# Gather, prefix sum and matmul on one core: four tiles' indices loaded directly, w loaded and cast in four parts, matmuls on zeros at the start, and the first and last pair of tiles handled singly

## The chip, the core and the metric

The kernel runs on one NeuronCore of a Trainium2 chip. The core has five engines that run their own instruction streams: TensorE (PE), VectorE (DVE), ScalarE (ACT), GpSimd (POOL) and SyncE (SP), and 16 DMA engines that move data between HBM and the on-chip memories. Engines wait for each other through semaphores. The metric is the device time of one execution in microseconds (us), as a median of several runs. A profile is taken of one execution; its "span" is the time from the first to the last instruction of the program, which is a little less than the execution's own time.

## What is computed

```python
B, S, N, D = (16, 4096, 2048, 512)      # x: B,S,D float32; indices: B,N int64, sorted; w: D,D float32
gathered = x[b_idx, indices, :]         # 2048 rows of each of the 16 batches
cs = np.cumsum(gathered, axis=1)        # running sum over the gathered rows, batch by batch
out = np.matmul(cs, w)                  # (16, 2048, 512) float32
```

So 67 MB of rows are read, 67 MB of results are written, and between them stand a running sum down each batch and a product with a 512 x 512 matrix.

## The kernel before, in words

The gathered rows are cut into tiles of 128 rows: 16 tiles to a batch, T = 256 tiles in all. Two neighbouring tiles are a *pair* (R = 2, G = 128 pairs). Each pair goes through these steps, each on its own engine:

- `gather(t)` on POOL: one indirect DMA per tile. 128 row numbers, one to a partition, pick 128 rows of 2 KB, which land in `g32` (eight buffers of a pair). POOL does nothing else after its set-up, so the gathers are issued one behind the other; a gather into a used buffer waits until the pair that was in it has been cast.
- `cast(g)` on ACT: the pair is cast from float32 to float16 (`g16`, four buffers). It waits for both tiles of the pair.
- `sums(t)` on PE: four 128x128 matmuls per tile against `ut`, a matrix of ones and zeros, leave the running sums inside the tile, transposed, in PSUM (`pa`, four buffers).
- `carry(t)` on DVE: adds the last column of the tile before (the total so far) and writes float16 to `cst`; the first tile of a batch is only copied.
- `project(g, j)` on PE: four 128x512 matmuls per tile against `w16` give the output rows in PSUM (`pb`, two buffers of a pair). It waits until both tiles of the pair have been carried and until the buffer has been drained.
- `drain(g)` on ACT: one copy of the pair, 128x1024, from PSUM to `ob` (eight buffers).
- `store(g)` issued by SP: one DMA of 512 KB to the output; each partition writes two neighbouring rows, 4 KB.

The order on each engine is written out by hand. PE runs AH = 2 pairs of sums ahead: it does the sums of pairs 0 and 1, and then `step(g)`: project tile 0 of pair g, sums of tile 0 of pair g+2, project tile 1 of pair g, sums of tile 1 of pair g+2. Most steps run in a loop of four. ACT does cast 0, the cast of w, casts 1 and 2, and then, for every g, cast g+3 and drain g. So the drain of pair g stands behind the cast of pair g+3, which waits for that pair's gathers.

Set-up before that: the row numbers arrive as int64. `idx64` holds the indices of all 256 tiles, one tile to a partition row (two loads of 128 tiles, KI = 2); DVE casts them to float32, PE transposes them, and DVE casts them back to integers in `idxg`, where one tile's indices lie one to a partition. Because this takes a while, the first FIRST = 2 tiles have their indices loaded straight into that form (`idx_first`, 256 separate elements of 8 bytes). w is loaded in one DMA of 1 MB behind the indices on SP's queue, and cast to float16 in one ACT instruction of 128x2048. POOL builds `ident` (for the transposes) and `ut`.

The semaphores that the change touches: `s_first`, `s_w` (landed loads), `s_wc` (w has been cast), `s_prep` (transposed indices ready), `s_c` (pairs cast), `s_b` (tiles projected), `s_d` (tiles carried), `s_e` (pairs drained).

Of the kernel before, what the change touches and what calls it, by code (L numbers as in the profile page):

```python
# [7 lines left out]
P = 128  # L8
FP32 = mybir.dt.float32
FP16 = mybir.dt.float16  # L10
U32 = mybir.dt.uint32
# [16 lines left out]
def kernel(  # L28
# [19 lines left out]
    FIRST = R  # L48
    NG = 16
    NH = 4  # L50
    NA = 4
    NB = 2
    NC = 4
    NO = 8
    LOOP = 4
    AH = 2
# [7 lines left out]
    idx_first = const.tile([P, FIRST, 2], U32)  # L64
# [4 lines left out]
    w16 = const.tile([P, DC, D], FP16)  # L69
    ut = const.tile([P, R, Q], FP16)  # L70
    ident = const.tile([P, P], FP32)
    g32 = [const.tile([P, R, D], FP32, name=f"g32_{i}") for i in range(NG // R)]
    g16 = [const.tile([P, R, D], FP16, name=f"g16_{i}") for i in range(NH)]
    cst = [const.tile([P, DC, R, P], FP16, name=f"cst{i}") for i in range(NC)]
# [6 lines left out]
    def sem(name):  # L81
        return tc.alloc_semaphore(name)

    s_first, s_w, s_ut, s_wc, s_if, s_pt, s_prep = (
        sem(f"s_{n}") for n in ("first", "w", "ut", "wc", "if", "pt", "prep")
    )
    s_idx = [sem(f"s_idx{k}") for k in range(KI)]
    s_g = [sem(f"s_g{i}") for i in range(NG)]
    s_o = [sem(f"s_o{i}") for i in range(NO)]
    s_c = sem("s_c")  # L90
# [8 lines left out]

    def gather(t):  # L100
        g, r = divmod(t, R)
        pool.need(s_c, g + 1 - NG // R)
        if t < FIRST:
            pool.need(s_first, 16)
            ap = idx_first[:, t, 0:1]
        else:
            pool.need(s_prep, t // P + 1)
            ap = idxg[:, t // P, t % P : t % P + 1]
        nc.gpsimd.indirect_dma_start(  # L109
            out=g32[g % (NG // R)][:, r, :],  # L110
            out_offset=None,
            in_=x_flat,
            in_offset=bass.IndirectOffsetOnAxis(ap=ap, axis=0),
            element_offset=(t // NT) * S * D,
        ).then_inc(s_g[t % NG], 16)

    def cast(g):
        for t in range(R * g, R * g + R):
            act.need(s_g[t % NG], 16 * (t // NG + 1))
        act.need(s_a, R * (g - NH + 1))  # L120
        nc.scalar.copy(out=g16[g % NH][:], in_=g32[g % (NG // R)][:]).then_inc(s_c, 1)  # L121

    def sums(t, first=0):
        g, r = divmod(t, R)
        if isinstance(first, int):
            pe.need(s_c, g + 1)
            pe.need(s_ut, 4)
            pe.need(s_d, t - NA + 1)
        elif r == 0:
            nc.tensor.wait_ge(s_c, first + (g + 1))  # L130
# [27 lines left out]

    def project(g, j, first=0):
        if isinstance(first, int):  # L160
            pe.need(s_wc, 1)
            pe.need(s_d, R * (g + 1))
            pe.need(s_e, g - NB + 1)
        elif j == 0:
            nc.tensor.wait_ge(s_d, R * first + R * (g + 1))
            nc.tensor.wait_ge(s_e, first + (g - NB + 1))
        for c in range(DC):
            mm = nc.tensor.matmul(  # L168
                out=pb[g % NB][:, j],
                lhsT=cst[g % NC][:, c, j, :],  # L170
                rhs=w16[:, c, :],
                start=(c == 0),
                stop=(c == DC - 1),
            )
        mm.then_inc(s_b, 1)

    def drain(g):
        act.need(s_o[g % NO], 16 * (g // NO))
        act.need(s_b, R * (g + 1))
        nc.scalar.copy(out=ob[g % NO][:], in_=pb[g % NB][:]).then_inc(s_e, 1)  # L180

    def store(g):
# [2 lines left out]
        sp.need(s_e, g + 1)  # L185
        nc.sync.dma_start(out=dst, in_=ob[g % NO][:]).then_inc(s_o[g % NO], 16)


    with nc.allow_non_contiguous_dma(reason="a few indices, one per partition"):
        nc.sync.dma_start(  # L190
            out=idx_first[:],
            in_=indices[0, 0 : FIRST * P].bitcast(U32).rearrange("(t p w) -> p t w", p=P, w=2),
        ).then_inc(s_first, 16)
    idx_rows = indices.bitcast(U32).rearrange("b (t q) -> (b t) q", q=2 * P)
    for k in range(KI):
        nc.sync.dma_start(
            out=idx64[:, k, :], in_=idx_rows[k * P : (k + 1) * P, :]
        ).then_inc(s_idx[k], 16)
    nc.sync.dma_start(out=w32[:], in_=w.rearrange("(c p) d -> p c d", p=P)).then_inc(s_w, 16)
    for g in range(G):  # L200
        store(g)
    for g in range(G - NO, G):
        sp.need(s_o[g % NO], 16 * (g // NO + 1))


    nc.gpsimd.memset(ident[:], 1.0).then_inc(s_ut, 1)  # L206
# [22 lines left out]
    nc.gpsimd.drain()  # L229


    for k in range(KI):
        dve.need(s_idx[k], 16)
        nc.vector.tensor_copy(out=idxf[:, k, :], in_=idx64[:, k, 0::2]).then_inc(s_if, 1)  # L234
    for k in range(KI):
        pe.need(s_ut, 3)
        pe.need(s_if, k + 1)
        nc.tensor.transpose(  # L238
            out=pb[k % NB][:, 0, :P], in_=idxf[:, k, :], identity=ident[:]
        ).then_inc(s_pt, 1)  # L240
# [24 lines left out]

    cast(0)
    act.need(s_w, 16)
    nc.scalar.copy(out=w16[:], in_=w32[:]).then_inc(s_wc, 1)  # L268
# [36 lines left out]
```

## Time and profile before

| | |
|---|---|
| median of 4 runs | 351.3 us (350.87 to 351.7) |
| the profiled execution, its own time | 350.85 us |
| its span | 349.1 us |
| PE / DVE / ACT / POOL busy | 86% / 51% / 73% / 70% of the span |
| data moved by DMA | 135.66 MB, mean 389 GB/s |
| first gather issued, last gather issued | 3.15 us, 322.13 us |
| first store issued, last store issued | 20.61 us, 344.92 us |

How to read it: a page gives busy times, the DMA rate in 40 equal slices of the span, and the chain of work that ended last. A row of a group reads: line, engine, operation, output <- input, count, then busy time in us and mean ns of one, then idle time in front of the group and what ended it. A row of the timeline reads: start in us, duration in us, engine, line, operation, and in brackets the idle time before it and what ended it; "x4" means that four instructions are merged. "DMA to landing" is the time from the issue of a DMA by its engine to its completion. "issue" is time in which the engine waited for nothing that the profile shows. A stretch row reads: from:to, length, then for each of PE, PE's weight loads, DVE, ACT and POOL the busy us and the number of instructions, then the granted TensorE clock, the mean busy share of the DMA engines, and GB/s. The matmuls' ends are modelled, so a busy PE is not necessarily PE at its peak.

### The profile page before, as it was taken

Reading aid. Unit: us, or ns where it says so; the run is one execution under the profiler, and the core shown is the slowest. Engines: PE = TensorE matmul, PEld = TensorE weight load, DVE = VectorE, ACT = ScalarE, POOL = GpSimd, SP = SyncE. Lnnn points to the kernel's source line nnn. Section 1 sums busy time; section 2 is a strip of 40 time slices with the busy share of each in tenths; the row PEclk is TensorE's granted clock in tenths of the full one; section 3 lists DMA queues with packets and bytes.
Section 4 is the critical chain, followed back from the end, with each engine's and each line's share of the span. In section 5 each row is a group of like instructions: output and inputs, shape, how many; then the busy total and the mean of one; then the engine's idle time right before and its main releaser. Section 6 shows DMA issues by size and latency. Waiting matters only on the chain.

```text
span 349.1 us, 6009 instructions
## 1 busy us (share of the span) xinstructions
PE 299.9 (86%) x2050; PEld 149.8 (43%) x2050; DVE 178.1 (51%) x260; ACT 253.2 (73%) x258; POOL 243.3 (70%) x264
## 2 busy tenths in 40 slices
PE   1398989899989999898898988989889989889883
PEld 0254444445444444444444434445434444445441
DVE  1354555456545555555554545555545555455550
ACT  0765877778778777777777767787778777778763
POOL 6777777777777777777777777777777777777000
PEclk9999999999999999999999999999999999999998
DMA  6789999999999999999999999999999999999945
GB/s 217 231 242 379 408 413 409 413 408 414 416 416 416 416 417 415 416 416 416 417 416 416 416 414 414 407 412 408 413 412 409 417 413 414 413 415 414 390 194 240
DMA packets 40012, 135.66 MB, mean 389 GB/s; under 512 B 6464, under 2 KB 6720, under 8 KB 40000
## 3 DMA queue, kind: packets, MB, share of 16 engines
q0 software_dynamic: 20480, 67.13, 49.3%
q1 hardware_dynamic: 19520, 68.43, 48.6%
q14 instruction: 11, 0.09, 0.1%
q8 instruction: 1, 0.02, 0.0%
HBM read 68.42 MB, written 67.11 MB: 388 GB/s over the span
## 4 chain that ended last, share of the span: by engine, by line
POOL 50%; DMA 23%; issue 19%; PE 3%; ACT 3%; POOLq 0%; SPq 0%; ACTq 0%
POOL g L109 50%; DMA g<-in_x_dram,idxg 22%; ACT g L121 3%; PE pb L168 3%; PE pa L132 1%; DMA idx_first<-in_indices_dram 1%; POOLq L229 0%; ACT ob L180 0%; SPq L300 0%; ACTq L23 0%; SPq L79 0%
## 5 line engine op out<-in xcount | busy, mean ns | idle before, releaser
L109 POOL DMA_INDIRECT g<-in_x_dram,idxg x254 | 240.1, 945 | 77.4 <-issue 72.8
L168 PE MATMUL pb<-w,cst 128*128 128x512 f16 x1024 | 263.4, 380 | 0.0
L152 DVE TENSOR_TENSOR cst<-pa,cst 128x512 f16<-128x512 f32 x240 | 166.0, 692 | 138.9 <-PE pa L132 137.9
L121 ACT CAST g<-g 128x1024 f16<-128x1024 f32 x128 | 133.5, 1045 | 76.3 <-issue 73.7
L132 PE MATMUL pa<-ut,g 128*128 128x128 f16 x1024 | 100.9, 222 | 39.8 <-ACT g L121 38.3
L180 ACT COPY ob<-pb 128x1024 f32<-128x1024 f32 x128 | 128.7, 1005 | 5.2 <-PE pb L168 5.2
L132 PEld LDWEIGHTS pa<-ut,g 128*128 128x128 f16 x1024 | 70.2, 99 | 127.5 <-ACT g L121 94.6
L168 PEld LDWEIGHTS pb<-w,cst 128*128 128x128 f16 x1024 | 89.9, 98 | 61.6 <-issue 0.8
L147 DVE CAST cst<-pa 128x512 f16<-128x512 f32 x16 | 11.1, 692 | 19.7 <-PE pa L132 19.7
L121 ACT ACT_TABLE_LOAD x1 | 1.3, 1283 | 10.2 <-DMA g<-in_x_dram,idx_first 10.2
L238 PE MATMUL pb<-ident,idxf 128*128 128x128 f32 x2 | 0.9, 462 | 4.1 <-DVE idxf L234 4.0
L109 POOL DMA_INDIRECT g<-in_x_dram,idx_first x2 | 2.1, 1042 | 1.5 <-DMA idx_first<-in_indices_dram 1.2
L234 DVE CAST idxf<-idx 128x128 f32<-128x128 uint32 x2 | 0.5, 226 | 4.1 <-DMA idx<-in_indices_dram 4.1
L238 PEld LDWEIGHTS pb<-ident,idxf 128*128 128x128 f32 x2 | 0.4, 182 | 4.4 <-issue 4.0
L268 ACT CAST w<-w 128x2048 f16<-128x2048 f32 x1 | 1.9, 1893 | 0.0
L243 DVE CAST idxg<-pb 128x128 uint32<-128x128 f32 x2 | 0.6, 291 | 0.3 <-PE pb L238 0.3
L206 POOL MEMSET ident<- 128x128 f32 x1 | 0.2, 204 | 0.5 <-SPq L79 0.5
L209 POOL TENSOR_SCALAR_AFFINE_SELECT ident<-ident 128x128 f32<-128x128 f32 x1 | 0.3, 286 | 0.1
L289 POOL MEMSET const-float32-0.0<- 128x1 f32 x1 | 0.1, 98 | 0.3 <-issue 0.3
L218 POOL TENSOR_SCALAR_AFFINE_SELECT ut<-ut 128x128 f16<-128x128 f16 x1 | 0.3, 289 | 0.0
L207 POOL MEMSET ut<- 128x128 f16 x1 | 0.2, 205 | 0.0
L289 POOL MEMSET const-uint8-127<- 128x1 uint8 x1 | 0.1, 115 | 0.0
(2 smaller groups left out, 0.2 us busy)
## 6 DMA issues: line engine op xcount, KB each, us to landing
out_dram<-ob SPq DMA_DIRECT2D x128, 512.0 KB, 7.1
g<-in_x_dram,idxg POOLq DMA_INDIRECT x254, 10.1
w<-in_w_dram SPq DMA_DIRECT2D x1, 1024.0 KB, 6.3
idx<-in_indices_dram SPq DMA_DIRECT2D x2, 128.0 KB, 2.2
g<-in_x_dram,idx_first POOLq DMA_INDIRECT x2, 5.5
idx_first<-in_indices_dram SPq DMA_DIRECT2D x1, 2.0 KB, 1.9
```

Of the source, the lines that this page charges most:

```text
L109: nc.gpsimd.indirect_dma_start(out=g32[g % (NG // R)][:, r, :], out_offset=None, in_=x_flat, in_offset=bass.IndirectOffsetOnAxis(ap=ap, ax ...
L121: nc.scalar.copy(out=g16[g % NH][:], in_=g32[g % (NG // R)][:]).then_inc(s_c, 1)
L132: mm = nc.tensor.matmul(out=pa[t % NA][:, c], lhsT=g16[g % NH][:, r, c * P : (c + 1) * P], rhs=ut[:], start=(c == 0), stop=(c == DC - 1),)
L147: nc.vector.tensor_copy(out=dst, in_=pa[t % NA][:]).then_inc(s_d, 1)
L152: nc.vector.tensor_tensor(out=dst, in0=pa[t % NA][:], in1=last.unsqueeze(2).broadcast_to([P, DC, R, Q]), op=mybir.AluOpType.add,).then_inc ...
L168: mm = nc.tensor.matmul(out=pb[g % NB][:, j], lhsT=cst[g % NC][:, c, j, :], rhs=w16[:, c, :], start=(c == 0), stop=(c == DC - 1),)
L180: nc.scalar.copy(out=ob[g % NO][:], in_=pb[g % NB][:]).then_inc(s_e, 1)
L209: nc.gpsimd.affine_select(out=ident[:], in_=ident[:], compare_op=mybir.AluOpType.is_equal, fill=0.0, base=0, pattern=[[-1, P]], channel_mu ...
L234: nc.vector.tensor_copy(out=idxf[:, k, :], in_=idx64[:, k, 0::2]).then_inc(s_if, 1)
L238: nc.tensor.transpose(out=pb[k % NB][:, 0, :P], in_=idxf[:, k, :], identity=ident[:]).then_inc(s_pt, 1)
L243: nc.vector.tensor_copy(out=idxg[:, k, :], in_=pb[k % NB][:, 0, :P]).then_inc(s_prep, 1)
L268: nc.scalar.copy(out=w16[:], in_=w32[:]).then_inc(s_wc, 1)
```

## The change

At the start:
- FIRST becomes 4: the indices of tiles 0 to 3 are loaded straight, in two loads, tiles 0 and 1 by SP's queue and tiles 2 and 3 by ACT's, each with its own semaphore.
- w is loaded in four DMAs of 256 KB, each with its own semaphore. ACT casts the first two parts and DVE the last two, each 128x512; a projection waits for all four.
- DVE first clears a small tile `zeros`; PE multiplies it with itself nine times ahead of the transposes and ten times behind them, into a PSUM buffer that nobody reads. ACT copies one column of `zeros` to `spare` before anything else.
- Pair 0 is cast as two single tiles, each with its own step of the new semaphore `s_c0`; the sums of tile 0 wait only for tile 0.
- The cast of w stands ahead of the first gathered tile on ACT, no longer behind it. PE does the sums of pair 0, then the projections of pair 0 alternating with the sums of pair 1, then the sums of pair 2, then the steps from pair 1 on.

At the end:
- The last pair is cast as two single tiles (`s_c1`).
- PE does both projections of pair 125 ahead of the sums of tile 254, and one projection of pair 126 between the sums of tiles 254 and 255.
- The last pair is drained in halves, 128x512 each, tile 254 by DVE and tile 255 by ACT, and stored in two DMAs of 256 KB with rows of 2 KB.

Between start and end the loop is as before; only the counts of `s_c` are shifted by one.

```diff
-    FIRST = R
+    FIRST = 2 * R
...
+    zeros = const.tile([P, D], FP16)
+    spare = const.tile([P, 1], FP16)
...
     def gather(t):
         g, r = divmod(t, R)
-        pool.need(s_c, g + 1 - NG // R)
+        if g >= NG // R:
+            pool.need(s_c0, R)
+            pool.need(s_c, g - NG // R)
         if t < FIRST:
-            pool.need(s_first, 16)
+            pool.need(s_first[g], 16)
...
+    def cast_tile(t, done):
+        g, r = divmod(t, R)
+        act.need(s_g[t % NG], 16 * (t // NG + 1))
+        act.need(s_a, R * (g - NH + 1))
+        nc.scalar.copy(out=g16[g % NH][:, r], in_=g32[g % (NG // R)][:, r]).then_inc(done, 1)
...
-            pe.need(s_c, g + 1)
+            if g in (0, G - 1):
+                pe.need(s_c1 if g else s_c0, r + 1)
+            else:
+                pe.need(s_c, g)
...
-            pe.need(s_wc, 1)
+            pe.need(s_wc, DC)
...
+    def drain_last(j, lane, copy):
+        g = G - 1
+        lane.need(s_o[g % NO], 16 * (g // NO))
+        lane.need(s_b, R * g + j + 1)
+        copy(out=ob[g % NO][:, j], in_=pb[g % NB][:, j]).then_inc(s_el[j], 1)
+
+    def store_last():
+        b, h = divmod(G - 1, GB)
+        dst = out[b, h * R * P : (h + 1) * R * P, :].rearrange("(p j) d -> p j d", j=R)
+        for j in range(R):
+            sp.need(s_el[j], 1)
+            nc.sync.dma_start(out=dst[:, j], in_=ob[(G - 1) % NO][:, j]).then_inc(s_ol[j], 16)
...
-        nc.sync.dma_start(
-            out=idx_first[:],
-            in_=indices[0, 0 : FIRST * P].bitcast(U32).rearrange("(t p w) -> p t w", p=P, w=2),
-        ).then_inc(s_first, 16)
+        for k, eng in enumerate((nc.sync, nc.scalar)):
+            t = k * R
+            eng.dma_start(
+                out=idx_first[:, t : t + R, :],
+                in_=indices[0, t * P : (t + R) * P]
+                .bitcast(U32)
+                .rearrange("(t p w) -> p t w", p=P, w=2),
+            ).then_inc(s_first[k], 16)
...
-    nc.sync.dma_start(out=w32[:], in_=w.rearrange("(c p) d -> p c d", p=P)).then_inc(s_w, 16)
-    for g in range(G):
+    for c in range(DC):
+        nc.sync.dma_start(out=w32[:, c, :], in_=w[c * P : (c + 1) * P, :]).then_inc(s_w[c], 16)
+    for g in range(G - 1):
         store(g)
+    store_last()
...
+    def busy(n):
+        pe.need(s_z, 1)
+        for _ in range(n):
+            nc.tensor.matmul(
+                out=pb[NB - 1][:, R - 1], lhsT=zeros[:, :P], rhs=zeros[:], start=True, stop=True
+            )
+
+    nc.vector.memset(zeros[:], 0.0).then_inc(s_z, 1)
...
+    busy(9)
     for k in range(KI):
         pe.need(s_ut, 3)
...
+    busy(10)
...
+    for c in range(DC // 2, DC):
+        dve.need(s_w[c], 16)
+        nc.vector.tensor_copy(out=w16[:, c, :], in_=w32[:, c, :]).then_inc(s_wc, 1)
     for t in range(T):
         carry(t)
+    drain_last(0, dve, nc.vector.tensor_copy)
...
-    for t in range(R * AH):
+    for t in range(R):
         sums(t)
     pe.need(s_prep, KI)
-    for g in range(LOOP):
+    for j in range(R):
+        project(0, j)
+        sums(R + j)
+    for t in range(2 * R, R * (AH + 1)):
+        sums(t)
+    for g in range(1, LOOP):
         step(g)
...
-    for g in range(G - LOOP, G):
+    for g in range(G - LOOP, G - AH - 1):
         step(g)
-
-
-    cast(0)
-    act.need(s_w, 16)
-    nc.scalar.copy(out=w16[:], in_=w32[:]).then_inc(s_wc, 1)
+    project(G - 3, 0)
+    project(G - 3, 1)
+    sums(T - 2)
+    project(G - 2, 0)
+    sums(T - 1)
+    project(G - 2, 1)
+    project(G - 1, 0)
+    project(G - 1, 1)
+
+
+    act.need(s_z, 1)
+    nc.scalar.copy(out=spare[:], in_=zeros[:, :1])
+    for c in range(DC // 2):
+        act.need(s_w[c], 16)
+        nc.scalar.copy(out=w16[:, c, :], in_=w32[:, c, :]).then_inc(s_wc, 1)
+    for t in range(R):
+        cast_tile(t, s_c0)
     for g in range(1, AH + 1):
         cast(g)
-    for g in range(G):
-        if g + AH + 1 < G:
+    for g in range(G - 1):
+        if g + AH + 1 < G - 1:
             cast(g + AH + 1)
+        elif g + AH + 1 == G - 1:
+            for t in range(T - R, T):
+                cast_tile(t, s_c1)
         drain(g)
+    drain_last(1, act, nc.scalar.copy)
```

More of the change, by code (lines that the diff above doesn't have):

```diff
@@ L82, in sem @@
         return tc.alloc_semaphore(name)
-    s_first, s_w, s_ut, s_wc, s_if, s_pt, s_prep = (
-        sem(f"s_{n}") for n in ("first", "w", "ut", "wc", "if", "pt", "prep")
-    )
+    s_z, s_ut, s_wc, s_if, s_pt, s_prep, s_c0, s_c1 = (
+        sem(f"s_{n}") for n in ("z", "ut", "wc", "if", "pt", "prep", "c0", "c1")
+    )
+    s_first = [sem(f"s_first{k}") for k in range(2)]
+    s_w = [sem(f"s_w{c}") for c in range(DC)]
     s_idx = [sem(f"s_idx{k}") for k in range(KI)]
+    s_el = [sem(f"s_el{j}") for j in range(R)]
+    s_ol = [sem(f"s_ol{j}") for j in range(R)]
     s_g = [sem(f"s_g{i}") for i in range(NG)]
@@ L129, in sums @@
         elif r == 0:
-            nc.tensor.wait_ge(s_c, first + (g + 1))
+            nc.tensor.wait_ge(s_c, first + g)
         for c in range(DC):
@@ L198 @@
         ).then_inc(s_idx[k], 16)
-    nc.sync.dma_start(out=w32[:], in_=w.rearrange("(c p) d -> p c d", p=P)).then_inc(s_w, 16)
-    for g in range(G):
+    for c in range(DC):
+        nc.sync.dma_start(out=w32[:, c, :], in_=w[c * P : (c + 1) * P, :]).then_inc(s_w[c], 16)
+    for g in range(G - 1):
         store(g)
-    for g in range(G - NO, G):
+    store_last()
+    for g in range(G - NO, G - 1):
         sp.need(s_o[g % NO], 16 * (g // NO + 1))
+    for j in range(R):
+        sp.need(s_ol[j], 16)
     nc.gpsimd.memset(ident[:], 1.0).then_inc(s_ut, 1)
@@ L252, in step @@
                 sums(R * (g + AH) + j, first)
-    for t in range(R * AH):
+    for t in range(R):
         sums(t)
     pe.need(s_prep, KI)
-    for g in range(LOOP):
+    for j in range(R):
+        project(0, j)
[3 more added lines that the diff above has]
+    for g in range(1, LOOP):
         step(g)
```

## The prediction

> **What bounds the kernel now.** I read the page's slices and the chain first, then the landing times of the gathers at four places, then both ends in order of time.
>
> ```profile
> GB/s 217 231 242 379 408 413 409 413 408 414 416 416 416 416 417 415 416 416 416 417 416 416 416 414 414 407 412 408 413 412 409 417 413 414 413 415 414 390 194 240
> POOL 50%; DMA 23%; issue 19%; PE 3%; ACT 3%; POOLq 0%; SPq 0%; ACTq 0%
> L109 POOL DMA_INDIRECT g<-in_x_dram,idxg x254 | 240.1, 945 | 77.4 <-issue 72.8
> ```
>
> The chain says POOL: 256 gathers, one every 1.25 us (0.95 busy, 0.30 issue), the first at 3.15 us, the last at 322.13. But the rate row says more. A pair of tiles is read (524,288 B) and written (524,288 B); at one pair per 2.5 us that asks for 419 GB/s, and the DMA moves 407 to 417. So it serves slightly less than POOL orders, and a queue must grow. It does: these are the landing times of gathers issued in 8 to 20, 24 to 50, 100 to 120 and 300 to 349 us.
>
> ```profile
> DMA to landing us min/median/max: 3.5/3.7/4.7
> DMA to landing us min/median/max: 6.5/7.7/8.0
> DMA to landing us min/median/max: 8.0/8.5/8.8
> DMA to landing us min/median/max: 14.4/14.8/15.6
> ```
>
> From 3.7 us with an empty queue to 15.6 at the end. The trace also records the sixteen partial completions of each gather: fifteen parts of the last one are in by 329.1 us and the sixteenth at 337.7. One of the 16 DMA engines is the last, and nothing in steady state waits for anything else.
>
> So the end is: the moment the DMA becomes fully loaded, plus the work in front of the last read, plus a tail. Before stores exist, the DMA is half idle (last column GB/s, the one before it the DMA's share):
>
> ```profile
> 12.00:16.00 4.00, 1.70 (x15) 1.44 (x16) 1.41 (x3) 4.00 (x4) 2.99 (x4) 1.00 0.70 216
> 16.00:20.00 4.00, 4.00 (x22) 2.06 (x20) 2.25 (x4) 1.59 (x3) 3.09 (x4) 1.00 0.71 210
> 20.00:24.00 4.00, 4.00 (x32) 2.32 (x31) 2.56 (x4) 3.57 (x5) 3.09 (x4) 1.00 0.89 261
> ```
>
> The first store is late because of this stretch: table load, cast 0, the whole of w on ACT, three casts, a slow first projection, the first drain.
>
> ```profile
> 10.19 1.28 ACT L121 ACT_TABLE_LOAD   x1 [10.19 <-DMA g<-in_x_dram,idx_first]
> 11.48 1.04 ACT L121 CAST g<-g 128x1024 f16<-128x1024 f32 x1
> 12.44 1.89 ACT L268 CAST w<-w 128x2048 f16<-128x2048 f32 x1
> 14.23 2.93 ACT L121 CAST g<-g 128x1024 f16<-128x1024 f32 x3
> 16.16 1.91 PE L168 MATMUL pb<-w,cst 128*128 128x512 f16 x4
> 19.58 1.01 ACT L180 COPY ob<-pb 128x1024 f32<-128x1024 f32 x1 [2.41 <-PE pb L168]
> 20.61 13.91 SPq L186 DMA_DIRECT2D out_dram<-ob  x6
> ```
>
> Check of the reading: store data flows from about 22.5 us (first store issued at 20.6, data 1.9 later). From there to the last landing at 337.7 are 315.2 us. In them lie 243 reads of 262,144 B and 123 stores of 524,288 B; at 414 GB/s these take 243 x 0.633 + 123 x 1.266 = 309.6 us, 98% of it. That stretch has almost no slack to lose or gain; only where it begins, and the tail, can move.
>
> **The change part by part.**
>
> *Four tiles' indices straight.* POOL's third gather already starts at 5.85 us with no wait beyond its 0.30, so this removes nothing; it moves the first use of the transposed indices from tile 2 (5.85) to tile 4 (8.35). The second load goes by ACT's queue beside SP's first. The first load's 8-byte packets ran from 2.09 to 2.54 us, so sharing can cost the first gather between 0 and 0.45; each packet took 9 ns, 16 to an engine, which leaves room, so I take 0.1.
>
> *Nineteen matmuls on zeros, transposes behind nine of them.* The DVE memset that they wait for lies between 0.20 us (POOL's memset of 128x128) and 0.69 (a DVE cast of 128x512): 0.4, ending at 1.4. Nine at the cold 0.43 to 0.48 us (1.91 for four at 16.16) end at 5.4 to 5.8. Two transposes (0.46 each) and one index cast (0.29) put the first indices at 6.2 to 6.6 against 8.35: 1.7 us of cover, cost nothing; were it gone, POOL's chain would slip one for one. Ten more end between 8.8 and 11; the first prefix sums can start at 10.1. What PE could lose there is below 1 us and is covered by 2 us (below).
>
> *w in four loads, casts on ACT and DVE.* SP issues three DMAs more, 0.43 to 0.47 us each, all before its first store. w was complete at 8.8 us and is the same bytes. ACT's two casts (a 1024-wide one takes 1.05, a 2048-wide one 1.89, so 0.62 each for 512) and DVE's two end near 9.5, when the first gather has just landed whole (9.46); the table load goes to the idle front. DVE's two casts run while POOL writes gathers. In the trace the one gather with such a DVE cast inside it (3.64) took 1.14 us, its neighbours 0.95: 0.19 for a cast of 0.23. Bounds: 0, and both casts in full, 2 x 0.69 = 1.4. I take the row, 0.2 in all, since it isn't certain that both fall inside a gather. The Trainium skill's "SBUF — State Buffer" (section "SBUF: two separate sides") warns that such a DVE copy locks GpSimd out, so that gathers cannot be written for its whole length; by that rule alone the term would be up to its upper end, 1.4, and the forecast 350.0.
>
> *First pair by single tiles, and the start.* Casts 0, 1, pair 1 and pair 2 now follow the landings (9.46, 10.12, 11.5, 13.7 us), and projection 0 ends near 14.2. On ACT the cast of pair 3 stands ahead of drain 0, so drain 0 waits for tile 7, which is issued at 12.10 and lands at 15.71 whatever the others do: 15.75 + 1.05 + 1.0 = 17.8, against 20.6. That is the 2 us of cover. From there store g follows the landing of pair g+3 by 2.05 us, as it does before from store 4 on (29.64, 31.66).
> Stores begin 2.8 us earlier, but reads are paced by POOL: 2.8/1.25 = 2.2 reads are still to come, 1.4 us of DMA work. The last landing moves by 2.8 - 1.4 = 1.4 us. Bounds: 0 (the DMA finds other holes, as in 24 to 28 us at 314 GB/s) and 2.8 (the whole shift). Less the two delays (0.1 + 0.2): 1.1.
>
> *Last pair by single tiles.* Times after the last landing L, before: cast 0.07 to 1.12, last sums to 2.65, two projections of pairs 126 and 127 to 6.12, drain to 7.2, store issued 7.23, its last packet 9.5, end of the span 11.4. After: tile 254 lands 1.2 us ahead and is cast before L; tile 255 is cast at 0.07 to 0.69; drain 124 then ends at 1.6 and frees the buffer for projection 126, whose first half runs 1.75 to 2.6; sums 255 to 2.85, second half to 3.7, projection 127 to 5.45. The halves are drained by DVE (4.65 to 5.35) and ACT (5.5 to 6.1), where before it was one copy of 1.01. The last store is issued at 6.15, 1.1 us sooner. It is half the size, but store 126 and the first half are still ahead of it: data ends near 8.1 instead of 9.5. Gain 1.4 (bounds 1.1, the issue alone, and 1.7, no queue).
>
> Between the ends the loop is the same, instruction for instruction, with counts shifted by one. **Sum:** 1.1 + 1.4 = 2.5 us. The profiled execution took 350.85 (span 349.1); the median of the four, 351.3, is 0.45 more, and the same 2.5 comes off it: **348.8 us**.
>
> **The rivals.**
>
> *Only the tail gains (349.9).* If the DMA isn't as continuously loaded as I say, earlier stores only fill holes that would have been filled later, and L stays: 351.3 - 1.4. For it: 24 to 28 us moved 314 GB/s with gathers already waiting 7.5 us. Against: the 98%.
>
> *The queue never builds (346.8).* Before, four drains came every 2.17 us (19.58, 21.75, 23.92, 26.10) and the landing time jumped from 3.7 to 7.5. After, they come at the reads' own 2.5 us. If that spares the jump, L moves by the whole 2.8, and with 1.7 in the tail: 351.3 - 4.5.
>
> *Slower: the transposes come late.* They stand behind nine matmuls in PE's queue, and gather 4 at 8.35 us and all later ones stand behind them. Cover is 1.7 us, and each us beyond it delays every gather. Against a gain of 2.5, it ends over 0.2% slower once the first indices are 1.7 + 2.5 + 0.7 = 4.9 us late, that is if nine matmuls take 8.9 us, 1.0 each. At 1.0 each: 352.0. The rows show 0.43 to 0.48, so this needs a price twice theirs.
>
> *No change:* the idle before the first store turns out to be hidden and the tail's gain is lost in stores queued in front of it: 351.0.
>
> **How the numbers follow.** 0.2% is 0.7 us, about what a measurement of this kernel can tell from none. My case 0.55; tail alone 0.19; no queue 0.12; no change 0.06; slower 0.08. Faster: 0.55 + 0.12 + 0.17 of the tail case (349.9 is near the border) = 0.84; same 0.08; slower 0.08. The range takes in the tail case with its smaller end (351.3 - 1.1 = 350.2, and 0.2 for the median's own scatter) and the no-queue case: 346.6 to 350.4.
>
> **What would show it.** Right: gathers start at 3.1 to 3.3 us and keep 1.25; the first store is issued near 17.8; gathers issued from 24 to 50 us land in 5.5 to 6.5 us instead of 7.7, those from 300 us in 13 to 14.5; from the last cast's end to the last store's issue 5.5 us instead of 6.1. Wrong: the first store after 19.5, a wait of POOL at tile 4, landings unchanged at 24 to 50 us (then only the tail can gain), or another engine that lags by more than 8.6 us.

## The result: no change that can be measured

The kernel after takes 351.4 us (median of 34 runs, 350.15 to 352.99), the kernel before 351.17 (55 runs, 350.31 to 352.65). The ratio is 1.0007, 95% interval 0.9999 to 1.0016. The forecast was 348.8 us, with a range that ended at 350.4. The profiled execution of after took 351.93 us (span 350.1), 0.5 over its own median; that of before took 350.85, 0.3 under its own. Where two single profiles are compared below, these differences have to be kept in mind.

The page of after, in the lines that answer to those shown of before: the DMA rate in 40 slices, the chain, the gathers.

```profile
GB/s 229 207 295 357 386 392 397 411 411 416 418 415 416 416 415 414 413 416 414 416 415 416 412 410 411 411 414 413 412 414 416 411 415 412 409 411 415 389 202 241
POOL 51%; DMA 25%; issue 18%; ACT 2%; PE 2%; POOLq 0%; SPq 0%; ACTq 0%
L117 POOL DMA_INDIRECT g<-in_x_dram,idxg x252 | 238.3, 946 | 76.8 <-issue 71.6
```

The third slice is faster (295 GB/s against 242), as the earlier stores should make it. But slices four to seven read 357, 386, 392, 397, where before had 379, 408, 413, 409. What was won in one slice was given back in four.

The time from issue to landing of the gathers issued in 8 to 20, 24 to 50, 100 to 120 and 300 to 349 us, kernel after:

```profile
DMA to landing us min/median/max: 3.5/3.7/6.5
DMA to landing us min/median/max: 5.6/8.2/9.2
DMA to landing us min/median/max: 9.4/9.8/10.1
DMA to landing us min/median/max: 15.2/16.2/16.7
```

The forecast asked for 5.5 to 6.5 us in the second line and 13 to 14.5 in the last. Both medians went up instead: from 7.7 to 8.2, and from 14.8 to 16.2.

The start itself went as planned. First the beginning of after in order of time, then what ACT does around the first stores:

```profile
1.47 4.02 PE L273 MATMUL pb<-zeros 128*128 128x512 f16 x9 [1.47 <-DVE zeros L277]
1.47 1.28 ACT L332 ACT_TABLE_LOAD   x1 [1.47 <-SPq L81]
3.36 1.14 POOL L117 DMA_INDIRECT g<-in_x_dram,idx_first  x1 [1.39 <-DMA idx_first<-in_indices_dram]
...
5.74 0.50 DVE L291 CAST idxg<-pb 128x128 uint32<-128x128 f32 x2 [1.08 <-PE pb L285]
...
7.13 0.43 DVE L294 CAST w<-w 128x512 f16<-128x512 f32 x1 [0.89 <-DMA w<-in_w_dram]
7.31 1.06 POOL L117 DMA_INDIRECT g<-in_x_dram,idx_first  x1 [0.30 <-issue]
...
8.66 0.48 DVE L294 CAST w<-w 128x512 f16<-128x512 f32 x1 [1.10 <-DMA w<-in_w_dram]
8.68 0.95 POOL L117 DMA_INDIRECT g<-in_x_dram,idxg  x1 [0.30 <-issue]
```

The table load lies in idle time, the transposed indices come in time, and the gather at 8.68, the first that needs them, has no wait beyond its usual 0.30. The first store is issued at 17.97 us instead of 20.61:

```profile
15.98 1.04 ACT L129 CAST g<-g 128x1024 f16<-128x1024 f32 x1 [1.22 <-DMA g<-in_x_dram,idxg]
16.94 1.00 ACT L197 COPY ob<-pb 128x1024 f32<-128x1024 f32 x1
18.64 1.04 ACT L129 CAST g<-g 128x1024 f16<-128x1024 f32 x1 [0.70 <-issue]
19.59 1.00 ACT L197 COPY ob<-pb 128x1024 f32<-128x1024 f32 x1
22.02 1.04 ACT L129 CAST g<-g 128x1024 f16<-128x1024 f32 x1 [1.42 <-issue]
22.97 1.00 ACT L197 COPY ob<-pb 128x1024 f32<-128x1024 f32 x1
26.62 1.04 ACT L129 CAST g<-g 128x1024 f16<-128x1024 f32 x1 [2.64 <-issue]
27.57 1.00 ACT L197 COPY ob<-pb 128x1024 f32<-128x1024 f32 x1
```

This view shows where the lead is lost. Each drain (COPY) follows a cast, and before each cast ACT is idle: 1.22, 0.70, 1.42 and 2.64 us. The cast at 26.62 is that of pair 6, tiles 12 and 13. The bracket says "issue", a wait that the profile can't name; the completions in the trace can: the last part of tile 13 lands at 26.55. In before it landed at 24.31, with its gather issued 0.33 us earlier, and the gather of tile 12 took 3.5 us there and 6.5 here, where two stores had been issued by then. So the stores, in us of issue, go:

| store | 1st | 2nd | 3rd | 4th | 5th | 6th | 7th | 8th | 9th | 10th |
|---|---|---|---|---|---|---|---|---|---|---|
| before | 20.61 | 22.79 | 24.96 | 27.14 | 31.69 | 34.19 | 36.86 | 38.73 | 41.42 | 44.04 |
| after | 17.97 | 20.62 | 24.0 | 28.6 | 30.54 | 33.18 | 35.04 | 38.52 | 43.6 | 46.22 |

The lead of 2.64 us has become a lag of 1.5 at the fourth store, comes back, and is a lag of 2.2 at the ninth and tenth. Before, pair 6 had landed (24.31) well ahead of the fourth store, so the first four stores follow each other every 2.17 us without waiting for a gather; the first such gap there is behind the fourth.

Stretches of 8 us (after 8 to 20), first after, then before; the last two columns are the mean busy share of the DMA engines and GB/s:

```profile
8.00:20.00 12.00, 7.60 (x59) 3.78 (x58) 6.01 (x9) 6.64 (x8) 8.95 (x11) 1.00 0.78 227
20.00:28.00 8.00, 4.72 (x36) 2.32 (x34) 2.77 (x4) 3.94 (x5) 6.17 (x7) 1.00 0.98 335
28.00:36.00 8.00, 7.94 (x60) 4.26 (x57) 4.85 (x8) 6.33 (x7) 6.05 (x7) 1.00 1.00 346
36.00:44.00 8.00, 4.45 (x30) 2.15 (x29) 2.76 (x4) 3.91 (x4) 5.99 (x7) 0.99 1.00 395
44.00:52.00 8.00, 8.00 (x49) 4.24 (x47) 4.05 (x6) 6.87 (x7) 6.17 (x7) 0.80 1.02 386
```

```profile
8.00:20.00 12.00, 5.70 (x34) 3.51 (x35) 3.66 (x6) 7.39 (x7) 8.95 (x11) 1.00 0.76 238
20.00:28.00 8.00, 8.00 (x59) 4.50 (x58) 5.18 (x8) 6.46 (x7) 6.17 (x7) 1.00 0.92 288
28.00:36.00 8.00, 6.04 (x43) 2.84 (x41) 3.62 (x6) 5.04 (x6) 5.87 (x8) 1.00 0.99 380
36.00:44.00 8.00, 7.68 (x55) 4.03 (x56) 4.50 (x7) 6.60 (x7) 6.17 (x7) 1.00 1.03 409
44.00:52.00 8.00, 7.10 (x50) 3.46 (x49) 4.21 (x7) 5.88 (x7) 5.97 (x7) 1.00 1.02 411
```

A DMA share of 1.00 is not full speed: at 28 to 36 us after shows 1.00 at 346 GB/s. The packets take longer. From 32 to 36 us a 4 KB packet of a gather took 233 ns on average in after and 184 in before, and from 100 us on, in before, it takes about 160. At 159 ns, the median there, 16 engines move 412 GB/s. So I count for each stretch the *hole*, its length times (1 - rate/412), and add the stretches from 8 to 80 us. Before has 8.27 us (5.07 of it up to 20 us, 3.20 behind), after 9.32 (5.39 and 3.93). The kernel with the earlier first store has the larger hole.

The rows of after hold a second difference: the granted TensorE clock is 0.80 from 44 to 52 us and 1.00 in before. A slower clock could delay stores too. But the fourth and the ninth store of after, at 28.60 and 43.6 us, are late ahead of that stretch. (In only the start, one of the kernels below, the clock is 0.57 from 28 to 36 us, but its late fourth store, at 30.45, waits for tile 13, which lands at 28.40.) And of the 36 executions of after on record, the seven with a mean clock of 0.997 or more, which leaves hardly any room for a dip, have a median of 351.4 us, as all have. (The twelve at 0.989 or less have 351.95, so part of the scatter may come from the clock.)

### The profile page after: what moved, and what is told of

Same layout as the page of the kernel before. It is cut to its first block, busy times and chain, and to the rows that moved or that the text cites. A ratio compares the mean times of both kernels' runs of the same rounds, so it can differ in the third digit from the quotient of the medians.

```text
span 350.1 us, 6060 instructions
## 1 busy us (share of the span) xinstructions
PE 304.9 (87%) x2069; PEld 152.0 (43%) x2069; DVE 180.1 (51%) x264; ACT 253.0 (72%) x262; POOL 243.5 (70%) x264
## 4 chain that ended last, share of the span: by engine, by line
POOL 51%; DMA 25%; issue 18%; ACT 2%; PE 2%; POOLq 0%; SPq 0%; ACTq 0%
POOL g L117 51%; DMA g<-in_x_dram,idxg 24%; ACT g L129 2%; PE pb L185 2%; DMA idx_first<-in_indices_dram 1%; PE pa L149 0%; ACT ob L209 0%; POOLq L267 0%; SPq L373 0%; ACTq L23 0%; SPq L81 0%
## 5 line engine op out<-in xcount | busy, mean ns | idle before, releaser
L129 ACT CAST g<-g 128x1024 f16<-128x1024 f32 x126 | 131.7, 1045 | 83.4 <-issue 78.0
L273 PE MATMUL pb<-zeros 128*128 128x512 f16 x19 | 6.6, 516 | 1.5 <-DVE zeros L277 1.5
L117 POOL DMA_INDIRECT g<-in_x_dram,idx_first x4 | 4.1, 1023 | 2.3 <-DMA idx_first<-in_indices_dram 1.4
L273 PEld LDWEIGHTS pb<-zeros 128*128 128x128 f16 x19 | 2.3, 127 | 4.6 <-issue 2.2
L135 ACT CAST g<-g 128x512 f16<-128x512 f32 x4 | 2.5, 619 | 1.8 <-DMA g<-in_x_dram,idx_first 1.5
L335 ACT CAST w<-w 128x512 f16<-128x512 f32 x2 | 1.2, 617 | 2.9 <-DMA w<-in_w_dram 2.9
L294 DVE CAST w<-w 128x512 f16<-128x512 f32 x2 | 0.9, 452 | 2.0 <-DMA w<-in_w_dram 2.0
```

What stands on the lines that cost most here:

```text
L117: nc.gpsimd.indirect_dma_start(out=g32[g % (NG // R)][:, r, :], out_offset=None, in_=x_flat, in_offset=bass.IndirectOffsetOnAxis(ap=ap, ax ...
L135: nc.scalar.copy(out=g16[g % NH][:, r], in_=g32[g % (NG // R)][:, r]).then_inc(done, 1)
L273: nc.tensor.matmul(out=pb[NB - 1][:, R - 1], lhsT=zeros[:, :P], rhs=zeros[:], start=True, stop=True)
L335: nc.scalar.copy(out=w16[:, c, :], in_=w32[:, c, :]).then_inc(s_wc, 1)
```

## The experiments

The question was whether the earlier first store brought nothing at all, or brought its gain and something else took it back. Two kernels take the halves of the change apart; two move the first store by holding PE back. They ran on one chip, with 29 runs of the kernel before (351.3 us) beside them.

**Only the end (e1_tail_only).** The kernel before with the single-tile casts and half drains of the last pair, and PE's order at the end; the start is before's.

```diff
+    project(G - 3, 1)
+    sums(T - 2)
+    project(G - 2, 0)
+    sums(T - 1)
...
+    drain_last(1, act, nc.scalar.copy)
```

> The kernel before with only the end of the change. Theory A (the head start of the stores is given back before 60 us, and only the tail gains): 0.5 to 0.9 us faster than before, since after the last landing the changed kernel needed 10.7 us where before needed 11.4. Theory B (the last landing follows from when the DMA gets its full load, as I predicted): the same here, 0.5 to 1.4 us faster, with the last landing unchanged at 336.5 to 338.5 us. If it isn't faster at all, the tail's gain is no gain.

Measured: 350.69 us (12 runs, 350.14 to 351.24), ratio 0.9983 (0.9971 to 0.9994). The end alone gains 0.6 us (0.2 to 1.0 by the interval), and no other version here has a lower median. Both theories asked for such a time, so this run does not part them; the last landing, 338.76 us, lies just above the range of theory B.

**Only the start (e2_start_only).** The kernel after with before's end.

```diff
-    for g in range(G - 1):
-        if g + AH + 1 < G - 1:
+    for g in range(G):
+        if g + AH + 1 < G:
...
-    drain_last(1, act, nc.scalar.copy)
```

> The changed kernel with the end of before. Theory A: no gain, 0 to 1.2 us slower than before (the whole change measured +0.2 with the tail's gain of some 0.7 in it); the store lead of 2.6 us at the first store is gone by the eighth. Theory B: 1.1 us faster than before.

Measured: 352.27 us (12 runs), ratio 1.0027 (1.001 to 1.0043). The start alone loses 1.0 us (0.4 to 1.5 by the interval), as theory A had it; theory B, a gain of 1.1, is out. With the 0.6 of the end that makes +0.4, and the whole change measured +0.2: the halves add up, and nothing takes the start's gain back later. It has none.

**The first store put back by PE alone (e3_late45).** More matmuls on zeros stand ahead of the first sums; all else of the start stays.

```diff
-    busy(10)
+    busy(45)
```

> The changed kernel with 45 in place of 10 matmuls on zeros behind the transposes, so that the first projections and with them the first store come some 3 us later, near 21 us, about where they were before. Theory A: within 0.5 us of the changed kernel, slower or faster. Theory B: 1.4 us slower than the changed kernel (3 us less store time, half of it DMA work).

Measured: 351.82 us (12 runs), ratio 1.0009 (0.9993 to 1.0026). That is 0.4 us over after's 351.4, within theory A's 0.5 and not theory B's 1.4. The first store is issued at 20.70 us, where before has it. Its stretches are before's again as well:

```profile
20.00:28.00 8.00, 7.66 (x58) 4.21 (x56) 6.05 (x9) 6.39 (x7) 6.17 (x7) 1.00 0.93 293
28.00:36.00 8.00, 7.86 (x57) 4.14 (x56) 4.82 (x8) 6.03 (x7) 5.87 (x8) 1.00 1.00 390
36.00:44.00 8.00, 6.93 (x49) 3.44 (x48) 4.05 (x7) 5.87 (x6) 6.17 (x7) 1.00 1.02 398
```

and the last gather lands at 337.81 us, as before's does (337.69). By that the kernel should have been about as quick as the one with the end alone, yet it took 1.1 us more. In its profile the loss is behind the last landing. The DMA from 340.5 to 349 us:

```profile
q1 hardware_dynamic: 692, 1.98, 59.5%
q8 instruction: 1, 0.02, 0.7%
issues: line engine op xcount, KB each, median us to landing
out_dram<-ob SPq DMA_DIRECT2D x2, 512.0 KB, 4.6
out_dram<-ob SPq DMA_DIRECT2D x2, 256.0 KB, 4.0
```

One packet of 16 KB of instructions is fetched at 341.5 us and takes 0.96 us on one DMA engine. The sixteenth part of each of the last four stores then comes 1.4 to 2.5 us behind the fifteenth, where the other five profiles show at most 0.04; the two half stores land in 4.0 us, not 2.6. The next two store packets that take longer than 200 ns, at 342.41 and 342.83 us, take 441 and 249 ns instead of about 160. With the fetch that is 1.3 us lost, and the very last part is 1.36 us late. The other kernels of this section fetch only once, at 22 to 30 us, with the one of the next test as the exception (23.8 and 41.5). The Trainium skill's "Runtime: NRT & Kernel Launch" (section "Terms") says that an engine's instruction memory is refilled in 16 KiB blocks; the packet has that size. That one engine did all three, and that the fetch delayed the stores, is read from these times; that the 35 more matmuls caused the fetch is not shown. No kernel was run that moves the fetch alone.

**The first store put back further (e4_late70).** As above with `busy(70)`.

> The same with 70 matmuls on zeros: first store near 26 us, 8 us later than in the changed kernel. Theory A: at most 1.5 us slower than the changed kernel, because PE and ACT then work off the pairs in a burst that fills the DMA. Theory B: 4 us slower.

Measured: 353.73 us (6 runs), ratio 1.0073 (1.0051 to 1.0095), +2.4 us over before and +2.3 over after. The first store is issued at 25.37 us. Its stretches from 20 to 36 us:

```profile
20.00:28.00 8.00, 6.21 (x53) 3.65 (x52) 5.11 (x8) 2.50 (x3) 6.17 (x7) 1.00 0.75 217
28.00:36.00 8.00, 8.00 (x60) 4.45 (x59) 5.23 (x8) 7.28 (x8) 5.87 (x8) 1.00 1.00 346
```

The measured +2.3 lies between the figures that the expectation gives for the two theories, and fits neither. So a late first store does cost time; an early one does not give it back. Now the profiles side by side, in us. "Last landing" is the last part of the last gather; "at the median" adds to it by how much the kernel's median differs from its profiled execution's time, which assumes that this difference arises before the landing. "Tile 12" is the time from issue to landing of its gather.

| kernel | first store | tile 12 | hole | last landing | at the median |
|---|---|---|---|---|---|
| before | 20.61 | 3.5 | 8.27 | 337.69 | 338.0 |
| only the end | 21.85 | 3.7 | 8.52 | 338.76 | 338.2 |
| after | 17.97 | 6.5 | 9.32 | 339.39 | 338.9 |
| only the start | 18.11 | 8.5 | 9.38 | 339.37 | 338.8 |
| e3_late45 | 20.70 | 4.5 | 8.24 | 337.81 | 338.0 |
| e4_late70 | 25.37 | 3.6 | 10.27 | 340.40 | 341.3 |

The last landing follows the hole: their difference is 329.4 to 330.2 in all six. (The hole was defined after the fact and is bookkeeping: it says how much time the DMA lost, not why.) Against the first store it has a lowest point, near 20.7 us, with a loss on both sides. Single landings scatter, as the second row shows, whose start is before's and whose landing is 1.1 us later; put to the median the three with a first store at 20.6 to 21.9 agree within 0.2 us, and the two at 18 within 0.1. POOL's later beginning (3.36 us instead of 3.15 in after) isn't the cause: only the start has 3.18 and the same last landing, and e3_late45 has 3.27 and before's.

The sixteen partial completions of a gather show which part of the DMA this is. Microseconds from the issue of a gather to its fifteenth and to its last part:

```
tile      24         64         96         128        192        255
before    5.9  7.4   7.4  8.0   8.5  8.7   8.6 10.1   7.2 13.3   7.0 15.6
after     7.4  9.1   8.0  8.6   7.5 10.1   7.6 11.1   6.9 14.3   6.9 16.9
```

Fifteen parts come within 6 to 9 us at tile 24 and still at tile 255; in these two kernels no queue grows on them. Only one falls behind, all the way. I read a part as the work of one of the 16 engines: after 329 us in before, the gathers' last 24 packets of 4 KB run one behind the other, never two at once. After's extra lag on this part (10.1 against 8.7) is there by tile 96 and is then kept to the end (1.0 to 1.4 us). On this reading the fifteen make up what they lose early, and the one never does. But the lag alone does not tell the kernels apart. Only the end, which starts as before does, shows 9.7 us at tile 96 and 16.4 at tile 255. At tile 255 the last part is behind the fifteenth by 8.6 us in before, 9.8 in only the end, 9.9 in after, 9.8 in only the start, 9.2 in e3_late45 and 8.1 in e4_late70, where the fifteenth itself takes 10.1. Nothing in the trace tells which engine moved a packet, so the hole above is that of all sixteen, a stand-in for that of the one.

**What stayed open.** Four more edits were to show directly whether the DMA's work sets the landing (half of every store left out), whether the order of ACT makes the hole (for the first eight pairs the drain ahead of the next cast), whether the second load queue and DVE's casts matter (both index loads on SP, all casts of w on ACT), and whether a burst of stores with the first ones held back does better (`hold`).

```diff
-        nc.sync.dma_start(out=dst, in_=ob[g % NO][:]).then_inc(s_o[g % NO], 16)
+        nc.sync.dma_start(out=dst[:, 0], in_=ob[g % NO][:, 0]).then_inc(s_o[g % NO], 16)
...
-        sp.need(s_e, g + 1)
+        sp.need(s_e, max(g + 1, 2))
```

The first pair of lines is the half store, the second the hold of two; the hold of three has a 3. The other two edits are told in words above.

Half the store, four times:

> The changed kernel, but of every pair but the last only the first of each partition's two rows is stored (half of the output stays unwritten). If the load of the DMA sets the last landing, then with three quarters of the bytes the gathers land 3.5 to 5 us after their issue to the end, the last one at 326 to 328 us, and the span is 337 to 340 us. If POOL or the processing chain set it, the span stays within 3 us of 350.

> The changed kernel, but of every pair but the last only the first of each partition's two rows is stored (half of the output stays unwritten). If the load of the DMA sets the last landing, then with three quarters of the bytes the gathers land 3.5 to 5 us after their issue to the end, the last one at 326 to 328 us, and the span is 337 to 340 us. If POOL or the processing chain set it, the span stays within 3 us of 350.

> The changed kernel, but of every pair but the last only the first of each partition's two rows is stored (half of the output stays unwritten). If the load of the DMA sets the last landing, then with three quarters of the bytes the gathers land 3.5 to 5 us after their issue to the end, the last one at 326 to 328 us, and the span is 337 to 340 us. If POOL or the processing chain set it, the span stays within 3 us of 350.

> The changed kernel, but of every pair but the last only the first of each partition's two rows is stored (half of the output stays unwritten). If the load of the DMA sets the last landing, then with three quarters of the bytes the gathers land 3.5 to 5 us after their issue to the end, the last one at 326 to 328 us, and the span is 337 to 340 us. If POOL or the processing chain set it, the span stays within 3 us of 350.

The drain ahead of the cast, twice:

> The changed kernel, but for the first eight pairs ACT drains pair g ahead of casting pair g+3, so that a finished pair's store does not wait for later gathers to land: first store near 15.8 us, 2 us earlier still. Theory A1 (the lead is lost because stores then wait for gathers, stop and go): fewer holes in the DMA between 28 and 60 us, and 0.5 to 1.5 us faster than the changed kernel. Theory A2 (a lead makes the load so even that the queue of gathers runs short, whatever the order on ACT): no faster than the changed kernel, within 0.5 us, or slower.

> The changed kernel, but for the first eight pairs ACT drains pair g ahead of casting pair g+3, so that a finished pair's store does not wait for later gathers to land: first store near 15.8 us, 2 us earlier still. Theory A1 (the lead is lost because stores then wait for gathers, stop and go): fewer holes in the DMA between 28 and 60 us, and 0.5 to 1.5 us faster than the changed kernel. Theory A2 (a lead makes the load so even that the queue of gathers runs short, whatever the order on ACT): no faster than the changed kernel, within 0.5 us, or slower.

One queue for the index loads and all casts of w on ACT, four times:

> The changed kernel without the two things that held POOL up by 0.2 to 0.35 us: the second index load goes by SP's queue behind the other index loads, and ACT casts all four parts of w. First gather back at 3.15 us, the fifth at 8.35. If those delays explain the start's loss of 1 us, it is 0.8 to 1.1 us faster than the changed kernel; if they only shift the gathers, 0.2 to 0.35 us faster; by theory A the rest of the loss stays.

> The changed kernel without the two things that held POOL up by 0.2 to 0.35 us: the second index load goes by SP's queue behind the other index loads, and ACT casts all four parts of w. First gather back at 3.15 us, the fifth at 8.35. If those delays explain the start's loss of 1 us, it is 0.8 to 1.1 us faster than the changed kernel; if they only shift the gathers, 0.2 to 0.35 us faster; by theory A the rest of the loss stays.

> The changed kernel without the two things that held POOL up by 0.2 to 0.35 us: the second index load goes by SP's queue behind the other index loads, and ACT casts all four parts of w. First gather back at 3.15 us, the fifth at 8.35. If those delays explain the start's loss of 1 us, it is 0.8 to 1.1 us faster than the changed kernel; if they only shift the gathers, 0.2 to 0.35 us faster; by theory A the rest of the loss stays.

> The changed kernel without the two things that held POOL up by 0.2 to 0.35 us: the second index load goes by SP's queue behind the other index loads, and ACT casts all four parts of w. First gather back at 3.15 us, the fifth at 8.35. If those delays explain the start's loss of 1 us, it is 0.8 to 1.1 us faster than the changed kernel; if they only shift the gathers, 0.2 to 0.35 us faster; by theory A the rest of the loss stays.

The kernel after once more beside them, twice:

> The changed kernel once more, for a second profile: how far the last landing and the holes in the DMA's work before 80 us scatter from one execution to the next. If the last landing follows the holes, it is 329.8 us plus the time that the DMA lost between 8 and 80 us, to within 0.5 us.

> The changed kernel once more, timed beside the others and for a second profile: how far the last landing and the holes in the DMA's work before 80 us scatter from one execution to the next. If the last landing follows the holes, it is 329.8 us plus the time that the DMA lost between 8 and 80 us, to within 0.5 us.

The first stores held back:

> The changed kernel, but SP sends the first store only when two pairs are drained, so stores 0 and 1 go together near 20.6 us instead of 17.97 and 20.62. Theory A: although one store is 2.6 us later, the holes before 80 us shrink from 9.3 to 8.3 to 9 us, and it is 0 to 1 us faster than the changed kernel. Theory B (every store earlier is a gain): 1.3 us slower than the changed kernel.

> The same with three pairs: stores 0, 1 and 2 go together near 23 us. Theory A: within 1 us of the changed kernel on either side. Theory B: 2.5 us or more slower than the changed kernel (5 and 2.5 us of delay for the first two stores, half of it DMA work).

These runs fell on chips where the kernel before itself took 440 to 465 us instead of 351, and so they say nothing on the question. There the granted clock was 0.87 to 0.90 in the profiled executions, against 0.98 to 1.00 above, and the last gather landed 4.5 to 6.7 us after its issue, not 16. In us, medians (each half store is one execution):

| edit | this | before beside it |
|---|---|---|
| half store (e5, e9, e13, e16) | 454.9, 457.6, 449.1, 462.6 | 455.9, 457.3, 451.1, 456.6 |
| drain first (e6, e10) | 456.3, 454.1 | 455.9, 457.3 |
| quiet (e7, e11, e14, e15) | 461.2, 460.8, 456.2, 454.9 | 455.9, 457.3, 457.3, 456.6 |
| after again (e8, e12) | 460.9, 457.4 | 455.9, 457.3 |
| hold of two, of three (e17, e18) | 456.7, 461.4 | 455.4 |

Taking away half of the written bytes gives no gain that can be told from the scatter there, so on those chips the DMA does not seem to be what bounds this kernel. The scatter is too wide for the question anyway: the ratio to before of one and the same edit, quiet, is 1.028 in e7 and 0.997 in e15. None of the four edits was tried under the conditions of the case.

## Why the prediction was wrong, step by step

**What bounds the kernel: half right.** The end is the last landing on one DMA engine plus a tail, and the landing follows how empty the DMA was early on. But "it serves slightly less than POOL orders, and a queue must grow" holds for one engine in sixteen only. And the check of 98%, from which "almost no slack to lose or gain" was read, overlooked that its own missing 2% are 5.6 us, over twice the 2.5 us that were forecast. In before 3.20 us of hole lie between 20 and 80 us already, 1.9 of them behind 22.5 us, where the check begins. There was something to lose. (The first packets of the first store move at 22.0 us, 1.4 us after its issue and not 1.9.)

**Four tiles' indices (taken at 0.1): right in size.** The first gather came at 3.36 us instead of 3.15, with the same start in another kernel at 3.18; so 0.0 to 0.2.

**Matmuls on zeros (taken at nothing): right.** The nine ended at 5.5 us (forecast 5.4 to 5.8), both index casts near 6.2 (forecast of the first indices 6.2 to 6.6), against a need at 8.68. The rival that the transposes come late is out.

**Casts of w on DVE (taken at 0.2): right, a little high.** The gather at 7.31 took 1.06 us instead of 0.95 with a cast of 0.43 beside it, the one at 8.68 took 0.95 with a cast of 0.48 over its first half. That is 0.1 in all. In e4_late70 such a cast lies wholly inside the gather at 7.12 us, in only the start inside that at 8.55, and both gathers take 0.95 all the same. And the row that the term was taken from, 1.14 us with a cast inside, was misread: it is the first gather, which takes 1.14 in every kernel here, in e8_after_again too, where the first DVE cast starts at 4.78 us, after that gather is over. The size came out by luck. The rule of the Trainium skill's "SBUF — State Buffer" (section "SBUF: two separate sides"), by which such a cast shuts GpSimd out for its whole length, would have made it up to 0.91; the measurement decides.

**First pair by single tiles: right up to the first store, and there the prediction failed.** The first store was forecast at 17.8 us and came at 17.97. The step that failed is the next: "The last landing moves by 2.8 - 1.4 = 1.4 us", with bounds of 0 and 2.8. It took for granted that the DMA stays full once the first store is out. In place of 1.4 less the two delays, a gain of 1.1 us, the start alone measured a loss of 1.0. The sentence "drain 0 waits for tile 7, which is issued at 12.10 and lands at 15.71 whatever the others do" is true of tile 7, and was then extended to all later pairs; but tile 12 lands in 6.5 us, not 3.5, once the first stores are out, and the fourth drain waits for it and tile 13. Before, the gathers become slow from tile 14 on (7.4 us), behind the first four drains' needs. The bound of 0 was wrong too: it excluded a loss for no reason that the profile gave. For a later first store the same arithmetic works fairly well: e4_late70 comes 4.76 us later, which is 4.76/1.25 x 0.633 = 2.4 us of reads already done, which leaves 2.4 us of loss; its last landing came 2.7 later (3.3 at the median).

That drains which wait for slowed gathers make the hole is argued from the order on ACT, the tile 12 column and the stores' times. The run that would have shown it, the drain ahead of the cast, is among those that can't be compared. Shown by time is that the start loses and the end gains. That the early first store is what loses is supported by e3_late45: it keeps the rest of the start, holds PE back, and gets before's hole and landing back, in one profile each. It does not hold back the store alone, since more gathered pairs have landed by the time the stores begin. The two holds of SP's stores would have parted these two, and they cannot be compared either.

**Last pair by single tiles: right mechanism, size too large.** Forecast 1.4 us (bounds 1.1 and 1.7), measured 0.6. The end of after in order of time:

```profile
339.41 0.62 ACT L135 CAST g<-g 128x512 f16<-128x512 f32 x1 [0.18 <-DMA g<-in_x_dram,idxg]
342.21 2.85 PE L185 MATMUL pb<-w,cst 128*128 128x512 f16 x12
344.30 0.69 DVE L209 COPY ob<-pb 128x512 f32<-128x512 f32 x1 [1.20 <-PE pb L185]
345.02 1.07 SPq L216 DMA_DIRECT2D out_dram<-ob  x2
345.15 0.58 ACT L209 COPY ob<-pb 128x512 f32<-128x512 f32 x1 [0.81 <-PE pb L185]
```

From the last landing (339.39) the last store is issued 6.37 us later (forecast 6.15, before 7.23), its last packet is through at 8.61 (forecast 8.1, before 9.5), and the span ends at 10.68 (before 11.44). So the issue gave 0.86 of the 1.1, and the half size gave nothing of the 0.3 hoped for. A part of the missing issue time is the price of four projecting matmuls: 1.03 us here, where the forecast had some 0.85. The rest is in the DMA. Its rate from 344.9 to 349.2 us in 40 slices, first after, then before, and the half stores' time to landing:

```profile
GB/s 0 0 267 305 419 495 305 457 419 343 419 457 343 495 248 286 381 438 400 343 381 420 381 343 381 419 381 229 0 0 0 0 0 0 0 0 0 0 0 0
GB/s 419 381 419 229 0 0 0 38 495 343 457 419 381 419 419 419 457 343 419 267 0 0 0 0 0 0 0 0 0 0 0 0 0 0 0 0 0 0 0 0
out_dram<-ob SPq DMA_DIRECT2D x2, 256.0 KB, 2.6
```

In before the DMA is idle in front of the last store's data. In after the data of store 126 and of both halves run on without a gap from 345.1 to 348.0 us, so the second half waits its turn behind the first. It lands in 2.6 us, as the last store of before did at twice the size, and its smaller size brings nothing.

**The rivals.** "No change" had the time (351.0) at a chance of 0.06, but by another way: its two gains vanish, whereas here a gain of 0.6 and a loss of 1.0 nearly cancel. "Only the tail gains" was right that earlier stores bring nothing, and wrong in that they cost nothing. "The queue never builds" is the reverse of what happened: the jump in landing times came sooner, with the first stores. Of the signs named as wrong, two appeared: landings at 24 to 50 us not shortened, and an engine that lags by more than 8.6 us (9.9 at the last gather: 339.39 less 329.44). From the last cast's end to the last store's issue it took 5.7 us, where 5.5 was forecast and before took 6.1.

## What to carry to other kernels

When a pipeline's reads and writes share the DMA and one engine's order ties each write to a later read, an earlier first write can slow the very reads that the next writes wait for; ask what the second to tenth write will wait for before counting the first one's lead as gain. A mean near capacity hides which engine is at capacity: look at the partial completions, and count lost time on the slowest alone. Measure the two ends of a change apart: here the end alone is worth 0.6 us and is the version to keep.

## What the runs showed of the hardware

- One of the sixteen parts of a gather, read as one of 16 DMA engines, fell behind by 8.1 us (e4_late70) to 9.9 us (after) over the span. The other fifteen came in 6 to 9 us in before and after, from tile 24 to tile 255. The Trainium skill's "DMA: Bandwidth & Descriptors" (section "Latency and other measured facts") says that two of the engines are usually slower when GpSimd issues the gathers; the completions here show one late part, not two, and can't name its engine.
- A DMA share of 1.00 went with 346 GB/s in one stretch and with 390 to 395 in others: busy DMA engines are not DMA engines at their rate.
- A fetch of 16 KB of instructions was one packet of 0.93 to 1.48 us in the six profiles. In the one profile where it fell among the last stores, their last parts were 1.4 to 2.5 us late.
- Two stores of 256 KB with rows of 2 KB, issued 0.74 us apart behind a store of 512 KB, landed in 2.6 us each, as one store of 512 KB with rows of 4 KB did in before. A packet of 2 KB took 86 ns and one of 4 KB about 160.
